# A decoder layer on one core: projection matmuls of the next unit queued on TensorE behind attention's matmuls of two steps before

## The chip, the core and the metric

The kernel runs on one core of a Trainium2 chip. Its time is the device time of one execution in microseconds (us), the median over the runs of a measurement. The engines are named as in the profile: PE (TensorE's matmuls) and PEld (its weight loads, which overlap with the matmuls), DVE (VectorE), ACT (ScalarE), POOL (GpSimd) and SP (SyncE, which issues nearly all DMAs). The order of the instructions on each engine is fixed when the program is built; an instruction that waits holds up all that stand behind it on that engine.

## What is computed

One decoder layer with 2048 tokens and a width of 1024, in float32. Of the reference this matters here:

```
proj = h @ w_in            # q,k,v of 8 forgetting ("fox") heads, q,k,v of 8 stick-breaking ("sb") heads, forget gates
o_fox = forgetting_attention(q_f, k_f, v_f, log_f)      # softmax(q.k/8 + F[t] - F[s]), s <= t
o_sb  = stick_breaking_attention(q_s, k_s, v_s)
    z = q.k/8;  rest = reversed exclusive cumsum of log_sigmoid(-z)
    a = exp(log_sigmoid(z) + rest), s < t;  o = a @ v
x = x + gate_a * (concat(head_rms_norm(o_fox), head_rms_norm(o_sb)) @ w_out)
x = x + gate_m * (silu(conv(h2 @ w_up)_gate) * conv(h2 @ w_up)_val) @ w_down
return rms_norm(x, g_final)
```

## The kernel before, in words

**Units.** The attention part is a list of 32 units (line 576): eight head pairs, first the four sb pairs, then the four fox pairs, and in each pair four blocks `tb` of 512 tokens. Below, "unit (1,2)" is the stick-breaking pair 1, token block 2, and "fox (0,2)" the forgetting pair 0, block 2. A unit's attention (`attend`, line 468) needs the unit's Q, K and V. They come from the unit's projection (`proj` and `finish_proj`, lines 341 and 283): 24 matmuls of 128x512 for q and 24 for k (line 281), and in even pairs 96 matmuls of 128x256 for the V of this pair and the next (line 320). Every product is made of three, since each factor is split in a high and a low part (`split`, line 43: a copy on ACT and a subtraction on DVE or POOL). When the accumulation of k is done, ACT copies its high part, DVE subtracts to get the low part (line 300), and four DMAs issued from SP put the two into the tile `K` (line 303). The V of odd pairs is loaded back from DRAM.

**Attention of an sb unit** goes by heads, and in a head by chunks of 512 keys from the diagonal to the left (`sb_head`, line 400). A chunk begins with the logits (two matmuls `ps_qk<-K,Q` for each of two query blocks, lines 378 and 379); the first chunk of a unit is the diagonal one, which needs the K that the unit's own projection has just made. Then ACT takes two sigmoids (410, 411), DVE a running product over the keys (the scans, 416 and 419), POOL or DVE a multiplication (420), PE transposes (388), ACT and DVE split the transposed weights (392, 393), and PE multiplies them with V (`ps_pv<-at,V`, line 397). So an sb unit goes around PE, ACT, DVE, POOL, PE, ACT, DVE, PE. A fox unit has no scans. A unit ends when DVE adds the last head's halves into `oT` (line 507).

**What sets the order.** The projection of the next unit runs beside the attention of this one. `interleave` (line 131) steps the generator `attend`, and after each step takes as many steps of `proj_gen(next unit)` as its share says (e[1] of n, line 136); what is left of the projection when attention has no more steps is drained at the end (line 142). That is the order in which the instructions are written. It is not yet the order on the engines: the program is built by a scheduler that goes by a model of the time, keeps the written order as a priority, and lets an instruction written later pass one that it takes to be still waiting. So where attention's next matmul is not ready in that model, PE is given projection matmuls, also those of the unit after the next and of the one after that, as far as the buffers go (10 tiles `hp` of activations, 5 tiles `K`, 6 tiles `V`, 2 banks for projections).

Of the kernel before, what the change touches and what calls it, by code (L numbers as in the profile page):

```python
# [1 line left out]

# [14 lines left out]
P = 128  # L17
# [16 lines left out]
def kernel(ctx: ExitStack, tc: tile.TileContext, x, c, w_ada, b_ada, g_attn, w_in, b_fgate,  # L34
                      g_out_fox, g_out_sb, w_out, g_mlp, w_up, conv_w, conv_b, w_down, g_final, out):
    nc = tc.nc
# [3 lines left out]
    def f(t):  # L40
        return t.bitcast(F32)
# [85 lines left out]
    def drain(g):  # L127
        for _ in g:
            pass

    def interleave(main, n, fillers):
        live = [[g, k, 0] for g, k, _ in fillers if g is not None]
        for i, _ in enumerate(main):
            tick()
            for e in live:
                while e[2] < (i + 1) * e[1] / n:
                    e[2] += 1
                    if next(e[0], StopIteration) is StopIteration:
                        e[2] = 1 << 30
        for g, _, whole in fillers:  # L140
            if g is not None and whole:
                drain(g)
# [3 lines left out]
    def open_pool(name, side=None, space=None):  # L146
        st = pools[name] = ExitStack()
        kw = dict(space=space) if space is not None else {}
        return st.enter_context(tc.tile_pool(name=name, bufs=1, side=side, reuse_waits="tile", **kw))
# [8 lines left out]
    sb = open_pool("sb", side="right")  # L158
# [25 lines left out]
    b = pv()  # L184
# [191 lines left out]
    def logits(cw, qcols, hl, Q, K):  # L376
        b = qk()
        nc.tensor.matmul(b[:, :cw], Q[:, hl, 0, qcols], K[:, hl, :cw], start=True, stop=False)  # L378
        nc.tensor.matmul(b[:, :cw], Q[:, hl, 1, qcols], K[:, hl, :cw], start=False, stop=True)  # L379
        return b  # L380

    def weighted(o, kts, blk, V, hl, first, last, diag):
        b = pt()
        at = sb.tile([P, 2, 2 * 2 * P], F32R, name="at", bufs=3)
        order = [(1, 0), (0, 0), (0, 1), (1, 1)]
        for i, (kk, qi) in enumerate(order):
            if not (diag and i == 0):
                nc.tensor.transpose(b[:, i * P:(i + 1) * P], blk(kts[kk], qi), ident)  # L388
        lo = P if diag else 0
        if diag:  # L390
            nc.scalar.activation(at[:, :, 0:P], edge[:, 0:2 * P].rearrange("p (a n) -> p a n", n=P), AF.Copy)
        nc.scalar.activation(at[:, 0, lo:], b[:, lo:], AF.Copy)  # L392
        nc.vector.tensor_sub(at[:, 1, lo:], b[:, lo:], f(at[:, 0, lo:]))  # L393
        for kk, kt in enumerate(kts):
            for w in range(2):
                rhs = at[:, w].rearrange("p (s q) -> p s q", q=P)[:, 0:4:3, :] if kk else at[:, w, P:3 * P]
                nc.tensor.matmul(o[:, 0:2 * P], V[kt // 4][:, kt % 4, hl, :], rhs,  # L397
                                 start=first and kk == 0 and w == 0, stop=last and kk == 1 and w == 1)

    def sb_head(j, qc, hl, Q, K, V, o):  # L400
# [61 lines left out]
    def tick(n=1):  # L462
        for d in deferred:
            d[1] -= n
        while deferred and deferred[0][1] <= 0:
            deferred.pop(0)[0]()
# [189 lines left out]
    lm = late_mod()  # L656
    Fbs = None
    tail = None
    for i, u in enumerate(units):
        kind, p, tb = u  # L660
        nxt = units[i + 1] if i + 1 < len(units) else None
        if u == ("sb", 1, 0):
            forget_sums()
        if u == ("fox", 0, 0):
            tick(1 << 20)
            close_pool("sx", "px")
            sx = open_pool("fx", side="right")
# [12 lines left out]
        if nxt is None:  # L680
            drain(lm)
            close_pool("sl", "psa")
            psc = open_pool("psc", side="right", space=PSUM)
            p2a = open_pool("p2a")
            loaded = [load_o(0, p) for p in range(3)]
            wo = []
            tail = first_mix(loaded)
        steps = nxt and (KT + 11 if nxt[:2] == ("sb", 0) else KT - 1 if nxt[1] % 2 else KT + 4)
        interleave(attend(kind, p, tb, results[kind, p], Fbs), n,
                   [(nxt and proj_gen(nxt), steps, True),  # L690
                    (lm if kind == "fox" and (p, tb) != (0, 0) else None, 4, False), (tail, 12, True)])
    drain(first_out())
    tick(1 << 20)
    for t in range(2, NTB):
# [188 lines left out]
    for sblk in range(2):  # L883
# [21 lines left out]
        a, b = bank_a(), bank_a()  # L905
# [44 lines left out]
    for tb in range(NTB):  # L950
# [12 lines left out]
        tail = []  # L963
# [57 lines left out]
```

## Time and profile before

| | us |
|---|---|
| median of 3 runs | 3142.17 |
| lowest and highest run | 3137.32, 3142.69 |
| the profiled execution | 3141.04 |
| its span from first to last instruction | 3139.3 |
| unit (0,3) of sb | 250.3 to 350.0 |
| units (1,0), (1,1), (1,2), (1,3) end at | 367.4, 404.1, 462.6, 533.9 |
| units (2,0), (2,1), (2,2), (2,3) end at | 553.2, 593.7, 653.3, 734.5 |
| units (3,0), (3,1), (3,2), (3,3) end at | 754.7, 796.7, 850.7, 922.0 |
| fox (0,0), (0,1), (0,2) end at | 959.7, 994.4, 1039.1 |
| the last fox unit ends at | 1602.0 |

The ends are those of the last `oT` addition of each unit (line 507). The rest of the span is the output projection and the channel mixer. A row of a view of stretches gives the stretch, its length, the busy time of each engine with its count of instructions, the granted TensorE clock as a share of full speed, and the share and rate of the DMA engines. A row of a timeline gives start, length, engine, line, operation, tiles and shapes, how many instructions are merged in it, and in brackets how long the engine stood idle before it and for whom. A row of waits gives who waited for whom, the total in us, how often, and the longest. Busy times of PE overlap in its pipeline, so a matmul's duration is longer than the distance from one start to the next.

### The profile page before, as it was taken

The page shows a single profiled execution, that of the slowest core. Times are in us where ns is not written, and L with a number is a line of the kernel's source. Part 1 is how long each engine was busy: PE and PEld are TensorE (multiplying, and loading weights), DVE is VectorE, ACT ScalarE, POOL GpSimd, SP SyncE. Part 2 cuts the span into 40 slices and gives each one's busy share as a digit, 9 for nine tenths or more (in the row PEclk, how much of TensorE's full clock was granted, in tenths as well). Part 3 has the DMA queues.
Part 4 walks back from the last instruction along what each step waited for, and adds up shares of the span by engine and source line. Part 5 has one row for each costly group of instructions (what it writes and reads, how often), then busy time and mean ns, then how long its engine had stood idle before and what let it go on. Part 6 is the DMA issues. An engine that isn't in the chain of part 4 may idle for free. (4 is left out here: it accounts for less than half of the span.)

```text
span 3139.3 us, 46425 instructions
## 1 busy us (share of the span) xinstructions
PE 2967.0 (95%) x15934; PEld 2511.6 (80%) x15934; DVE 2145.5 (68%) x3342; ACT 1691.0 (54%) x3161; POOL 1227.1 (39%) x1387
## 2 busy tenths in 40 slices
PE   6889998989989999999999999999899998999998
PEld 5778787877878889888877678888678887888887
DVE  6787888878875876556843587778987776354253
ACT  5666776666756676567744444444444444343332
POOL 1554455456553242242212344344444442322321
PEclk8999999999999999999999999999999999999999
DMA  9547542555336696585446632222222223554552
GB/s 267 177 140 255 168 136 69 182 185 155 123 108 221 214 314 211 158 313 162 164 158 222 212 97 86 86 83 83 82 82 89 85 81 130 190 199 161 189 199 90
DMA packets 292940, 496.51 MB, mean 158 GB/s; under 512 B 29448, under 2 KB 177664, under 8 KB 291680
## 3 DMA queue, kind: packets, MB, share of 16 engines
q1 hardware_dynamic: 281072, 480.92, 47.9%
q10 hardware_dynamic: 11632, 12.63, 1.1%
q8 instruction: 126, 2.06, 0.3%
q14 instruction: 110, 0.90, 0.1%
HBM read 352.61 MB, written 90.51 MB: 141 GB/s over the span
## 5 line engine op out<-in xcount | busy, mean ns | idle before, releaser
L810 PE MATMUL ps_o<-oa,wu 128*128 128x512 f32 x2088 | 503.5, 392 | 14.4 <-DVE oa L45 6.9
L810 PEld LDWEIGHTS ps_o<-oa,wu 128*128 128x128 f32 x2088 | 390.5, 188 | 105.5 <-DVE oa L45 10.7
L397 PE MATMUL ps_pv<-at,V 128*128 128x256 f32 x2304 | 410.9, 296 | 41.6 <-DVE at L393 24.8
L393 DVE TENSOR_TENSOR at<-ps_pt,at 128x512 fp32r<-128x512 f32 (+1 forms) x576 | 366.0, 653 | 102.8 <-ACT at L392 99.8
L281 PE MATMUL ps_pj<-hp,w_qk 128*128 128x512 f32 x1512 | 418.4, 406 | 11.1 <-ACT hp L44 3.1
L420 POOL TENSOR_TENSOR a<-a,r 128x512 f32<-128x512 f32 (+3 forms) x240 | 283.4, 1182 | 368.8 <-DVE r L416 112.3
L392 ACT ACTIVATE at<-ps_pt 128x512 fp32r<-128x512 f32 (+1 forms) x576 | 319.4, 577 | 179.8 <-PE ps_pt L388 147.3
L397 PEld LDWEIGHTS ps_pv<-at,V 128*128 128x128 f32 x2304 | 337.0, 192 | 84.6 <-DVE at L393 42.8
L281 PEld LDWEIGHTS ps_pj<-hp,w_qk 128*128 128x128 f32 x1512 | 275.7, 191 | 65.4 <-POOL hp L45 4.0
L45 DVE TENSOR_TENSOR wd<-wdraw,wd 128x1024 fp32r<-128x1024 f32 x88 | 112.4, 1277 | 261.4 <-ACT wd L44 261.4
L378 PE MATMUL ps_qk<-K,Q 128*128 128x512 f32 (+2 forms) x640 | 264.1, 414 | 11.3 <-DMA K<-q 5.8
L419 DVE TENSOR_TENSOR_SCAN r<-r 128x513 f32<-128x513 f32 x192 | 258.0, 1355 | 21.7 <-ACT r L410 14.5
L45 POOL TENSOR_TENSOR g<-graw,g 128x512 fp32r<-128x512 f32 x84 | 141.3, 1684 | 326.8 <-ACT g L44 326.8
L960 PE MATMUL ps_o<-wd,g 128*128 128x512 f32 x1040 | 250.8, 391 | 8.8 <-ACT g L44 8.8
L810 PE MATMUL ps_t<-ob,wu 128*128 128x512 f32 x984 | 243.2, 392 | 0.0
L320 PE MATMUL ps_pj<-w_v,hp 128*128 128x256 f32 (+1 forms) x1536 | 234.1, 291 | 4.8 <-DVE q L45 2.2
L379 PE MATMUL ps_qk<-K,Q 128*128 128x512 f32 (+2 forms) x640 | 238.1, 373 | 0.0
L960 PEld LDWEIGHTS ps_o<-wd,g 128*128 128x128 f32 x1040 | 196.2, 189 | 50.0 <-ACT g L44 9.2
L44 ACT ACTIVATE wu<-wuraw 128x512 fp32r<-128x512 f32 x214 | 133.2, 626 | 185.5 <-PE ps_o L810 111.5
L320 PEld LDWEIGHTS ps_pj<-w_v,hp 128*128 128x128 f32 x1536 | 211.8, 193 | 15.5 <-DVE q L45 3.1
L810 PEld LDWEIGHTS ps_t<-ob,wu 128*128 128x128 f32 x984 | 186.2, 189 | 39.4 <-DVE wu L45 0.3
L388 PE MATMUL ps_pt<-edge,a 128*128 128x128 f32 x1088 | 187.3, 281 | 27.6 <-POOL a L420 14.7
(217 smaller groups left out, 5743.3 us busy)
## 6 DMA issues: line engine op xcount, KB each, us to landing
hp<-hs SPq DMA_DIRECT2D x224, 512.0 KB
wuraw<-in_w_up_dram SPq DMA_DIRECT2D x84, 512.0 KB
wdraw<-in_w_down_dram SPq DMA_DIRECT2D x84, 512.0 KB
Q<-q SPq DMA_DIRECT2D x128, 256.0 KB
g<-u SPq DMA_DIRECT2D x42, 512.0 KB
graw<-g SPq DMA_DIRECT2D x84, 256.0 KB
hs<-hp SPq DMA_DIRECT2D x32, 512.0 KB
K<-q SPq DMA_DIRECT2D x128, 128.0 KB
```

The source lines that it names most:

```text
L45: (lo_engine or nc.gpsimd).tensor_sub(lo, src, f(hi))
L281: nc.tensor.matmul(acc, w[kt][:, a, n], h[:, bb], start=kt == 0 and i == 0, stop=kt == KT - 1 and i == 2)
L320: nc.tensor.matmul(av[:, t * width:(t + 1) * width], hts[kt][:, a, tok], w[1][kt][:, bb, 0:width], start=kt == 0 and m == 0, stop=kt == KT ...
L378: nc.tensor.matmul(b[:, :cw], Q[:, hl, 0, qcols], K[:, hl, :cw], start=True, stop=False)
L379: nc.tensor.matmul(b[:, :cw], Q[:, hl, 1, qcols], K[:, hl, :cw], start=False, stop=True)
L392: nc.scalar.activation(at[:, 0, lo:], b[:, lo:], AF.Copy)
L393: nc.vector.tensor_sub(at[:, 1, lo:], b[:, lo:], f(at[:, 0, lo:]))
L397: nc.tensor.matmul(o[:, 0:2 * P], V[kt // 4][:, kt % 4, hl, :], rhs, start=first and kk == 0 and w == 0, stop=last and kk == 1 and w == 1)
L419: nc.vector.tensor_tensor_scan(rev, rev, rev, 1.0, ALU.mult, ALU.bypass)
L420: (nc.vector if (ch + qi) % 4 == 0 else nc.gpsimd).tensor_mul(a[:, :need], a[:, :need], r[:, 1:need + 1])
L810: nc.tensor.matmul(b, w[:, p, j], o[:, q], start=first and i == 0, stop=last and i == 2, skip_group_check=True)
L960: nc.tensor.matmul(banks[t][n], g[:, a, t * P:(t + 1) * P], w[:, b, n * TB:(n + 1) * TB], start=k == 0 and i == 0, stop=k == NKD - 1 and i ...
```

## The change

While `interleave` takes steps of the fillers in a unit of the sb pairs 1, 2 and 3, each instruction that a filler puts on PE gets an edge to one matmul of attention, and so stands behind it in PE's order. That matmul is the last one that attention had issued two steps before (`marks[max(0, i - 2)]`; lines 378 to 379 and 397 note it in `latest`). The edge makes no instruction wait at run time; it binds only the order on PE. What is drained after the last step of attention gets no edge. Units of sb pair 0 and of fox stay as they were, and no instruction is added, removed or resized. Lines of the changed file from 143 on stand 5 to 8 lines further down: 281 is 288, 320 is 327, 378 and 379 are 385 and 386, 388 is 395, 397 is 404, 303 is 310.

```diff
+    latest = [None]
+
+    def interleave(main, n, fillers, paced=False):
         live = [[g, k, 0] for g, k, _ in fillers if g is not None]
+        marks = []
         for i, _ in enumerate(main):
             tick()
+            marks.append(latest[0])
             for e in live:
                 while e[2] < (i + 1) * e[1] / n:
                     e[2] += 1
-                    if next(e[0], StopIteration) is StopIteration:
+                    with tc.issue_after(marks[max(0, i - 2)].ins) if paced else nullcontext():
+                        done = next(e[0], StopIteration) is StopIteration
+                    if done:
                         e[2] = 1 << 30
...
-        nc.tensor.matmul(b[:, :cw], Q[:, hl, 1, qcols], K[:, hl, :cw], start=False, stop=True)
+        latest[0] = nc.tensor.matmul(b[:, :cw], Q[:, hl, 1, qcols], K[:, hl, :cw], start=False, stop=True)
...
-                nc.tensor.matmul(o[:, 0:2 * P], V[kt // 4][:, kt % 4, hl, :], rhs,
+                latest[0] = nc.tensor.matmul(o[:, 0:2 * P], V[kt // 4][:, kt % 4, hl, :], rhs,
...
-                    (lm if kind == "fox" and (p, tb) != (0, 0) else None, 4, False), (tail, 12, True)])
+                    (lm if kind == "fox" and (p, tb) != (0, 0) else None, 4, False), (tail, 12, True)],
+                   kind == "sb" and p > 0)
```

The built order of PE moves in the stretch from unit (0,3) to fox (0,3) and is the same, instruction for instruction, before and behind it. Three places follow, before and changed.

On PE, where unit (1,0) ends and (1,1) begins (`ps_qk<-K,Q` are logits, `ps_pj<-hp,w_qk` projections of q and k, `ps_pv<-at,V` the product with V); before:

```order
L379 MATMUL ps_qk<-K,Q 128x512
L485 MATMUL ps_pt<-headsel,sq 128x2 x2
L378 MATMUL ps_qk<-K,Q 128x512
L379 MATMUL ps_qk<-K,Q 128x512
L397 MATMUL ps_pv<-at,V 128x256 x8
L388 MATMUL ps_pt<-edge,a 128x128 x3
L378 MATMUL ps_qk<-K,Q 128x256
L379 MATMUL ps_qk<-K,Q 128x256
L378 MATMUL ps_qk<-K,Q 128x256
L379 MATMUL ps_qk<-K,Q 128x256
L388 MATMUL ps_pt<-edge,a 128x128 x4
L397 MATMUL ps_pv<-at,V 128x256 x8
```

The last row is the last product with V of unit (1,0); the logits above it are those of (1,1), three chunks of which have been begun by then. At the same place in the changed kernel:

```order
L492 MATMUL ps_pt<-headsel,sq 128x2 x2
L404 MATMUL ps_pv<-at,V 128x256 x8
L288 MATMUL ps_pj<-hp,w_qk 128x512 x18
L404 MATMUL ps_pv<-at,V 128x256 x8
L385 MATMUL ps_qk<-K,Q 128x256
L386 MATMUL ps_qk<-K,Q 128x256
L385 MATMUL ps_qk<-K,Q 128x256
L386 MATMUL ps_qk<-K,Q 128x256
L288 MATMUL ps_pj<-hp,w_qk 128x512 x6
```

Here the second `x8` is the end of unit (1,0). The 18 matmuls above it end the projection of k for unit (1,1), and the first logits of (1,1), which read that K, stand behind the end of (1,0). No logits of (1,1) stand ahead of it.

On PE, where unit (2,0) ends and (2,1) begins (`ps_pj<-w_v,hp` are projections of V); before:

```order
L397 MATMUL ps_pv<-at,V 128x256 x8
L388 MATMUL ps_pt<-edge,a 128x128 x3
L378 MATMUL ps_qk<-K,Q 128x256
L379 MATMUL ps_qk<-K,Q 128x256
L320 MATMUL ps_pj<-w_v,hp 128x256 x4
L378 MATMUL ps_qk<-K,Q 128x256
L388 MATMUL ps_pt<-edge,a 128x128 x2
L379 MATMUL ps_qk<-K,Q 128x256
L320 MATMUL ps_pj<-w_v,hp 128x256 x15
L388 MATMUL ps_pt<-edge,a 128x128 x5
L397 MATMUL ps_pv<-at,V 128x256 x8
```

Logits of (2,1), V matmuls and the last work of (2,0) stand in turn. In the changed kernel:

```order
L395 MATMUL ps_pt<-edge,a 128x128 x4
L404 MATMUL ps_pv<-at,V 128x256 x3
L327 MATMUL ps_pj<-w_v,hp 128x256 x36
L404 MATMUL ps_pv<-at,V 128x256 x8
L327 MATMUL ps_pj<-w_v,hp 128x256 x60
L385 MATMUL ps_qk<-K,Q 128x256
L386 MATMUL ps_qk<-K,Q 128x256
L385 MATMUL ps_qk<-K,Q 128x256
L386 MATMUL ps_qk<-K,Q 128x256
```

Now 96 V matmuls of unit (2,1), the whole V projection, stand between the last transposes of (2,0) and the first logits of (2,1), with only the end of (2,0) among them.

On SP, around the DMAs that fill K for unit (1,1) (`os` is the output of a finished unit, here (1,0), `hp` the next activations); before:

```order
L346 DMA hp<-hs_1_61 128x1024
L303 DMA K<-q_3908 64x512 x4
L307 DMA V<-vs_sb_2_210 128x1024
L293 DMA Q<-q_3907 64x1024 x4
L307 DMA V<-vs_sb_3_211 128x1024
```

and in the changed kernel:

```order
L353 DMA hp<-hs_1_85 128x1024
L310 DMA K<-q_3908 64x512 x2
L516 DMA os_0_112<-oT 128x512
L310 DMA K<-q_3908 64x512 x2
L300 DMA Q<-q_4285 64x1024 x4
```

The second half of K for (1,1) now stands behind the store of the output of (1,0), and the Q that follows is that of unit (1,2).

More of the change, by code (lines that the diff above doesn't have):

```diff
@@ L1 @@
-from contextlib import ExitStack
+from contextlib import ExitStack, nullcontext
 import concourse.bass as bass
@@ L129, in drain @@
             pass
-    def interleave(main, n, fillers):
+    latest = [None]
+    def interleave(main, n, fillers, paced=False):
         live = [[g, k, 0] for g, k, _ in fillers if g is not None]
+        marks = []
         for i, _ in enumerate(main):
             tick()
+            marks.append(latest[0])
             for e in live:
```

## The prediction

> **What bounds the kernel now.** I read the page first, then the stretches by unit, then the waits in the sb units.
>
> ```profile
> span 3139.3 us, 46425 instructions
> PE 2967.0 (95%) x15934; PEld 2511.6 (80%) x15934; DVE 2145.5 (68%) x3342; ACT 1691.0 (54%) x3161; POOL 1227.1 (39%) x1387
> ```
>
> Over the span PE is the busy engine. But the share is an average, and the built order of PE moves only from unit (0,3) to the start of fox (0,3). These are the sb units from (0,3) on, the three with tb = 3 in them, and fox (0,0) to (0,2):
>
> ```profile
> 250.30:922.00 671.70, 613.48 (x3867) 532.95 (x3866) 561.29 (x753) 456.00 (x997) 348.99 (x517) 0.98 0.48 150
> ...
> 462.60:533.90 71.30, 58.63 (x363) 49.20 (x362) 66.02 (x84) 49.93 (x110) 42.43 (x59) 0.95 0.28 90
> 653.30:734.50 81.20, 70.27 (x415) 58.79 (x414) 67.90 (x84) 52.77 (x114) 43.62 (x62) 0.98 0.45 146
> 850.70:922.00 71.30, 58.36 (x354) 49.23 (x353) 59.60 (x72) 45.30 (x94) 40.31 (x49) 0.95 0.28 86
> 922.00:1039.10 117.10, 113.80 (x774) 103.18 (x773) 72.39 (x198) 75.91 (x154) 41.86 (x58) 0.99 0.66 205
> ```
>
> Busy times stand in the order PE, PEld, DVE, ACT, POOL. In the fox stretch PE has 113.8 of 117.1 us and DVE 72.4: PE alone sets the time. In the sb stretch PE has 613 of 672 and DVE 561, and in the three tb = 3 units PE stands idle for 12.7, 10.9 and 12.9 us while DVE has .926, .836 and .836 of the time (66.02/71.30 and so on). That idle 36.5 us is what there is to fill. Who waits for whom in the sb stretch:
>
> ```profile
> ACT at L392 <- PE ps_pt L388: 91.3, 80, 5.3
> ...
> DVE at L393 <- ACT at L392: 33.8, 44, 4.1
> DVE oT L507 <- ACT o L506: 15.1, 11, 3.7
> ...
> PE ps_pv L397 <- DVE at L393: 21.3, 29, 1.3
> PE ps_pt L388 <- POOL a L420: 14.7, 20, 1.9
> ```
>
> It is a ring. PE waits for DVE and POOL, DVE for ACT, and ACT for PE. No wait is long, since the attention of a unit overlaps with that of the next: PE's order at the end of (1,0) has logits of (1,1) ahead of the last product with V.
>
> **The change part by part.** Its own run took 3141.0 us (3139.3 of span and 1.7 around it), 1.1 under the median 3142.2. I sum against 3141.0. No instruction is added; what changes is where 189 projection matmuls stand, and what stands at the units' ends.
>
> *Work that goes from sb to fox.* I counted the projection matmuls in PE's order by unit. From (0,3) to (3,3) 712 of q and k and 589 of V stand before, 624 and 488 in the changed order. So 88 and 101 go over to fox (0,0) to (0,2). Two runs and the groups of the page price them:
>
> ```profile
> 344.73 3.34 PE L281 MATMUL ps_pj<-hp,w_qk 128*128 128x512 f32 x14
> ...
> 544.15 1.82 PE L320 MATMUL ps_pj<-w_v,hp 128*128 128x256 f32 x14
> ...
> L281 PE MATMUL ps_pj<-hp,w_qk 128*128 128x512 f32 x1512 | 418.4, 406 | 11.1 <-ACT hp L44 3.1
> ...
> L320 PE MATMUL ps_pj<-w_v,hp 128*128 128x256 f32 (+1 forms) x1536 | 234.1, 291 | 4.8 <-DVE q L45 2.2
> ```
>
> A run of 14 lasts 13 distances and one duration: (3.34 - .41)/13 = .225 us for q and k, (1.82 - .29)/13 = .118 for V. 88 x .225 + 101 x .118 = 19.8 + 11.9 = 31.7 us, and at the fox stretch's 117.1 us for 113.8 of PE, **+33 us** there. Nothing hides it; PE is full. Before, this work lay under DVE's time in sb.
>
> *What sb gives back.* PE loses 31.7 us there, but DVE keeps its 561 us; few of its instructions change sides. So the length is 561.3 over the share that DVE can have, plus the stretches in which the new order leaves it nothing. The share is bounded by the units in which PE was not full: at best .926 as in (1,3), 606 us; at worst .865, the three tb = 3 units together (193.52/223.80), 649 us. Two things pull: fewer long rows of projections ahead of attention's transposes help (ACT's 91.3 us of waiting), and the tb = 3 units, now with 139 projection matmuls in (1,3) and (3,3) in place of 50 and 60, come to look like (2,3), which had 95 and .836. I take the middle, .895, 627 us: **-45 us** against 671.7.
>
> *The new ends of units: K.* In the changed order the k projection of (1,1) ends just ahead of the last eight products with V of (1,0), and the first logits of (1,1) stand right behind those. The trace shows one such chain, at the first unit:
>
> ```profile
> 60.62 0.60 ACT L44 ACTIVATE q<-ps_qk 128x512 fp32r<-128x512 f32 x1 [0.26 <-PE ps_qk L281]
> ...
> 63.27 0.68 DVE L45 TENSOR_TENSOR q<-ps_qk,q 128x512 fp32r<-128x512 f32 x1
> ...
> 65.80 2.30 SPq L303 DMA_DIRECT2D K<-q  x2
> ...
> 70.15 0.39 PE L378 MATMUL ps_qk<-K,Q 128*128 128x256 f32 x1 [3.59 <-DMA K<-q]
> ...
> 70.69 0.28 ACT L410 ACTIVATE r<-ps_qk 128x128 f32<-128x128 f32 x1 [1.68 <-PE ps_qk L379]
> ...
> 71.07 0.43 DVE L416 TENSOR_TENSOR_SCAN r<-r,edge 128x129 f32<-128x129 f32 x1 [3.04 <-ACT r L410]
> ```
>
> The copy takes .60, the subtraction .68, two issues 2.30, and the last of them lands after 70.15 - 68.10 = 2.05 us; then .54 to the sigmoid and .38 to the first scan. That is 5.6 us from the last k matmul to the logits, 6.5 to DVE's scan. Ahead of the waiting logits on PE stand only the eight products with V (1.11 us):
>
> ```profile
> 360.20 1.11 PE L397 MATMUL ps_pv<-at,V 128*128 128x256 f32 x8
> ```
>
> Behind them six projection matmuls, held by the edge, and all of (1,1). On SP the second half of K also stands behind the store of `oT`, under 1 us more. So PE stands 4.5 us and DVE, which has the K subtraction and one `oT` in that time, about 5. The order has this at four ends, into (1,1), (1,2), (3,1) and (3,2). Into (1,3), (3,0) and (3,3) PE has 3.4 to 4.7 us of work between the last k matmul and the first logits, but no logits stand ahead of the last product with V either: 3 us each. 4 x 5 + 3 x 3 = **29 us**; at least half is sure, by the missing overlap alone.
>
> *The new ends of units: V.* In pair 2 the V projections that are left when attention has no more steps are drained together, ahead of the next unit's attention in the written order. Into (2,1) 96 of them stand between the last transposes and the first logits, 96 x .118 = 11 us in which DVE gets only the V splits; into (2,2) 68, 8 us; into (2,3) 25, 3 us. Together **22 us**. So in even pairs V is not spread at all.
>
> *The clock.* In unit (1,0) the granted clock was .93 of full, though no single wait of PE in it was longer than 1.15 us:
>
> ```profile
> 350.00:367.40 17.40, 15.05 (x84) 12.48 (x83) 14.41 (x26) 12.73 (x33) 6.52 (x17) 0.93 0.95 303
> ...
> 364.32 0.44 PE L388 MATMUL ps_pt<-edge,a 128*128 128x128 f32 x2 [1.15 <-DVE at L393]
> ```
>
> .07 of 17.4 is 1.2 us of PE's clock lost. With 1.2 at each of the ten new ends, 12 at most, and nothing where DVE sets the pace behind them, I put **+3**. The Trainium skill, "TensorE: Matmul & The Clock Gate", Part 1, says that the clock halves after an idle window of about 3.4 us; by that the four K ends alone would halve it, once each, which is an estimate of 4 x 1.7 = 7 us in place of the 3. The row here shows a loss behind a shorter wait, and the measurement decides.
>
> The sum: 33 - 45 + 29 + 22 + 3 = +42. **3141 + 42 = 3183 us.** With the best share and all else it is 3141 + 33 - 66 + 51 = 3159; with the worst share and the clock at 12, 3141 + 33 - 23 + 51 + 12 = 3214.
>
> **The rivals.**
>
> *The gaps close (faster).* PE is the engine with most to do, its idle 36.5 us in the tb = 3 units get the projections, and the next unit's logits find their K in time because the edges bind order only and the steps before were spread. For it: PE's 95%, and that (1,3) had only 50 projection matmuls. Then DVE runs at .926 with no stretches lost: 33 - 66 = -33, 3108 us. Against it: DVE has .926 in (1,3) already, so a filled PE there gains little; and the order shows the ends. The Trainium skill, "Perfetto Trace Analysis", Identifying the Most-Contended Engine, says to take the engine of highest occupancy and to optimize it first; by that this rival is the likely one. It decides if DVE's idle time per unit end stays under 1 us.
>
> *The gain and the loss meet.* The share is .926 and only half of the 51 us at the ends is lost: 33 - 66 + 26 = -7, 3134 us; a little more loss, and it is no change at all.
>
> *Much slower.* The share falls to .836, that of (2,3) and (3,3), since the edges keep PE from running ahead in every unit: 561.3/.836 = 671 us, so 33 + 0 + 51 + 12 = +96, 3237 us. Against it: ACT's and DVE's waits behind long rows of projections get fewer.
>
> That the change does nothing is excluded, since the order differs over sixteen units.
>
> **How the numbers follow.** A measurement of this kernel can tell about 0.2%, 6 us, from no change. I give my forecast, 3150 to 3218, a chance of .74; the gaps closing .08; the meeting .11, of which .08 counts as within 0.2% and .03 as faster; much slower .07. So faster .11, same .08, slower .81. The range leaves out the closed gaps and the much slower case, 1.5 in 10: 3134 to 3218. The likeliest time is that of the sum, 3183.
>
> **What would show it.** In the changed profile: the stretch from the end of (3,3) to the end of fox (0,2) some 33 us longer, PE full in it; a wait of PE for `DMA K<-q` of 3 to 5 us at four ends of units, 12 to 20 us together, where the sb stretch now has none so long; DVE idle for about 10 us across the end of (2,0), with PE in a row of V matmuls; and sb from 250 us on between 660 and 700 us long. I am wrong if the sb stretch is under 640 us: then DVE had the projections to thank for its waits, and the ends cost little. I am wrong in the first term if the fox stretch grows by less than 25 us.

## The result and the profile after

| | before | changed |
|---|---|---|
| median, us | 3139.74 | 3273.99 |
| lowest and highest, us | 3136.12, 3142.69 | 3270.84, 3277.67 |
| ratio, with its 95% interval | | 1.0422 (1.0408 to 1.0435) |

The change makes the kernel slower by 134 us, 4.2%. The sign was forecast; the size was not: 3183 was given, with 3134 to 3218 as the range. The busy times are the same work in a longer span, from the page of the changed kernel:

```profile
span 3275.9 us, 46402 instructions
...
PE 3019.5 (92%) x15934; PEld 2543.3 (78%) x15934; DVE 2158.4 (66%) x3342; ACT 1689.5 (52%) x3162; POOL 1239.2 (38%) x1387
```

The span grew by 136.6 us. Two stretches hold nearly all of it: sb from the end of (0,2) to the end of (3,3), and fox (0,0) to (0,2). The changed kernel's view of stretches (length, then PE, PEld, DVE, ACT, POOL, clock, DMA share and rate):

```profile
250.70:1022.70 772.00, 629.80 (x3680) 535.48 (x3679) 564.43 (x745) 450.25 (x990) 361.38 (x517) 0.91 0.39 119
1022.70:1169.20 146.50, 143.63 (x952) 129.62 (x950) 77.15 (x201) 77.95 (x160) 42.17 (x58) 1.00 0.72 229
```

sb is 100.3 us longer with the same 561 to 564 us of DVE work. Fox is 29.4 longer, with PE full and 178 more matmul records. The rest of attention adds 3 us, and what follows it 3.5.

Where in sb is it? I cut a stretch of 20 us, from 8 before to 12 behind the end of each unit from (1,0) to (3,2), eleven stretches, and asked for the busy times in them. In the changed kernel, the end of (3,0) and the sum of the eleven:

```profile
809.40:829.40 20.00, 9.90 (x40) 8.31 (x40) 3.32 (x7) 3.49 (x10) 1.11 (x5) 0.67 0.64 206
...
sum 220.00, PE 154.74 PEld 132.96 DVE 81.58 ACT 78.28 POOL 42.67; mean PE 14.07 PEld 12.09 DVE 7.42 ACT 7.12 POOL 3.88
```

The same sum in the kernel before:

```profile
sum 220.00, PE 210.15 PEld 187.07 DVE 186.09 ACT 159.55 POOL 112.66; mean PE 19.10 PEld 17.01 DVE 16.92 ACT 14.50 POOL 10.24
```

DVE stands idle for 138.4 of the 220 us, before for 33.9: **104.5 us more, which is all that sb lost**. Outside of these stretches DVE's idle time fell from 76.5 to 69.2 us, and its own work grew by 3.1 (104.5 - 7.3 + 3.1 = 100.3). No engine of the ring got more to do; they stand and wait. In the end of (3,0) all four engines of the ring are idle for half of the time and more; before, the same end reads:

```profile
746.70:766.70 20.00, 18.43 (x112) 15.43 (x111) 14.49 (x23) 15.01 (x38) 15.01 (x24) 1.00 0.57 138
```

What they wait for there, by the waits of the changed kernel in sb:

```profile
ACT r L417 <- PE ps_qk L386: 110.5, 61, 12.7
...
DVE r L423 <- ACT r L417: 61.0, 14, 12.7
PE ps_qk L385 <- DMA K<-q: 54.4, 7, 12.3
...
DVE r L426 <- ACT r L417: 34.1, 22, 4.1
...
DVE V L45 <- ACT V L44: 16.7, 13, 3.0
```

Before, DVE's first scan waited 6.4 us for ACT in all of sb, and no row there has PE waiting for K:

```profile
DVE r L416 <- ACT r L410: 6.4, 10, 2.1
```

Now PE waits for K seven times, up to 12.3 us, and ACT's sigmoid and DVE's scan wait behind it. One of the seven, the end of (1,1), in the changed kernel's timeline:

```profile
395.86 12.04 SPq L353 DMA_DIRECT2D hp<-hs  x8
...
404.64 2.91 PE L288 MATMUL ps_pj<-hp,w_qk 128*128 128x512 f32 x12
...
407.39 1.11 PE L404 MATMUL ps_pv<-at,V 128*128 128x256 f32 x8
407.58 0.60 ACT L44 ACTIVATE q<-ps_pj 128x512 fp32r<-128x512 f32 x1 [2.32 <-PE ps_pj L288]
408.21 1.46 SPq L310 DMA_DIRECT2D K<-q  x2
408.22 0.69 DVE L45 TENSOR_TENSOR q<-ps_pj,q 128x512 fp32r<-128x512 f32 x1 [2.54 <-ACT q L44]
...
410.49 1.29 SPq L310 DMA_DIRECT2D K<-q  x2
417.85 0.58 PE L385 MATMUL ps_qk<-K,Q 128*128 128x256 f32 x1 [9.36 <-DMA K<-q]
...
419.13 1.17 DVE L423 TENSOR_TENSOR_SCAN r<-r,edge 128x129 f32<-128x129 f32 x2 [9.76 <-ACT r L417]
```

The last k matmuls of the projection stand just ahead of the last product with V, as the forecast had it. But eight loads of `hp` are issued ahead of K, and the last DMA of K, issued by 411.78, is not there before 417.85: 6.1 us. The forecast had taken 2.05 from the first unit. There only four DMAs of Q, 256 KB each, stood between the halves of K and two loads of weights, 128 KB each, just ahead of it; a load of `hp` has 512 KB. The loads of weights in the kernel before:

```profile
59.43 0.84 SPq L256 DMA_DIRECT2D raw_v<-in_w_in_dram  x2
```

At the end of (1,1) DVE is idle for 9.8 us.

### The profile page after: what moved, and what is told of

Same layout as the page of the kernel before. It is cut to its first block, busy times and chain, and to the rows that moved or that the text cites. A ratio compares the mean times of both kernels' runs of the same rounds, so it can differ in the third digit from the quotient of the medians.

```text
span 3275.9 us, 46402 instructions
## 1 busy us (share of the span) xinstructions
PE 3019.5 (92%) x15934; PEld 2543.3 (78%) x15934; DVE 2158.4 (66%) x3342; ACT 1689.5 (52%) x3162; POOL 1239.2 (38%) x1387
## 5 line engine op out<-in xcount | busy, mean ns | idle before, releaser
L404 PE MATMUL ps_pv<-at,V 128*128 128x256 f32 x2304 | 421.4, 302 | 49.7 <-DVE at L400 28.2
L288 PE MATMUL ps_pj<-hp,w_qk 128*128 128x512 f32 x1512 | 425.8, 417 | 7.6 <-ACT hp L44 3.0
L288 PEld LDWEIGHTS ps_pj<-hp,w_qk 128*128 128x128 f32 x1512 | 288.6, 200 | 65.1 <-POOL hp L45 4.0
L385 PE MATMUL ps_qk<-K,Q 128*128 128x512 f32 (+2 forms) x640 | 271.4, 425 | 72.1 <-DMA K<-q 60.1
L426 DVE TENSOR_TENSOR_SCAN r<-r 128x513 f32<-128x513 f32 x192 | 265.0, 1388 | 49.7 <-ACT r L417 34.8
L417 ACT ACTIVATE r<-ps_qk 128x512 f32<-128x512 f32 (+2 forms) x320 | 174.4, 545 | 148.7 <-PE ps_qk L386 119.4
L386 PE MATMUL ps_qk<-K,Q 128*128 128x512 f32 (+2 forms) x640 | 242.4, 380 | 0.0
L327 PE MATMUL ps_pj<-w_v,hp 128*128 128x256 f32 (+1 forms) x1536 | 225.8, 290 | 1.7 <-DVE q L297 1.7
```

Of the source, the lines that this page charges most:

```text
L288: nc.tensor.matmul(acc, w[kt][:, a, n], h[:, bb], start=kt == 0 and i == 0, stop=kt == KT - 1 and i == 2)
L327: nc.tensor.matmul(av[:, t * width:(t + 1) * width], hts[kt][:, a, tok], w[1][kt][:, bb, 0:width], start=kt == 0 and m == 0, stop=kt == KT ...
L386: latest[0] = nc.tensor.matmul(b[:, :cw], Q[:, hl, 1, qcols], K[:, hl, :cw], start=False, stop=True)
L404: latest[0] = nc.tensor.matmul(o[:, 0:2 * P], V[kt // 4][:, kt % 4, hl, :], rhs, start=first and kk == 0 and w == 0, stop=last and kk == 1 ...
L426: nc.vector.tensor_tensor_scan(rev, rev, rev, 1.0, ALU.mult, ALU.bypass)
```

## The experiments

Three explanations were put against each other, and the expectations call them by letters. A: the loss is made at the ends of units, above all by K that comes late behind the loads on SP. B: those loads matter little. C: the edges slow attention inside the units. Later two more came: E, that the lower clock behind the long waits costs time, against F, that it costs none; and G, that the missing overlap of two units is enough by itself. All diffs are against the changed kernel. A time is compared with the kernel before on the same chip, whose median was 3144 to 3147 us there (3140 on the chip of the result above), so ratios are safer to compare between runs than times. All kernels compute the whole layer.

**The loads behind K, in all units.**

```diff
...
-                nc.sync.dma_start(f(K[r * HD:(r + 1) * HD, h]), f(k2[h * HD:(h + 1) * HD, r]))
+                last_k[0] = nc.sync.dma_start(f(K[r * HD:(r + 1) * HD, h]), f(k2[h * HD:(h + 1) * HD, r]))
...
-            nc.sync.dma_start(f(h), hs[tb][kt])
+            with tc.issue_after(last_k[0].ins):
+                nc.sync.dma_start(f(h), hs[tb][kt])
```

> Edit: in the changed kernel, the loads of the activations hp for a projection stand on SP behind the DMAs that fill K of the projection before. The result after the change is 3274.0 us; in its trace PE waits 54.4 us for K at seven unit ends, 4 to 12 us each, where 3 to 5 us were forecast, and up to eight hp loads of 512 KB are issued on SP in the 12 us ahead of K. Theory A (queue): K's packets stand behind those of the hp loads in the same queue, so a landing takes 6 us and not 2. Then the waits for K fall to about 3 to 4 us each, 20 to 28 us together, and the time to 3230 to 3248. Rival B (the missing overlap alone): the ends cost what they cost because no logits stand ahead of them, and K lands late whatever stands in the queue. Then the waits stay over 45 us and the time is within 3262 to 3282.

3273.29 us, ratio 1.041 (1.039 to 1.0431): no gain in all. But sb fell by 31 us to 741.1, and PE's waits for K in it from 54.4 to 24.6 us; the edge also held the loads in fox, where the three units and those behind them grew by 24 us together. The run had mixed two things and decided nothing, so it was repeated with the edge in sb alone.

**The loads behind K, in sb alone.**

```diff
...
-            nc.sync.dma_start(f(h), hs[tb][kt])
+            with tc.issue_after(last_k[0].ins) if kind == "sb" and (p, tb) > (1, 0) else nullcontext():
+                nc.sync.dma_start(f(h), hs[tb][kt])
```

> Edit: as the run in which the hp loads stand behind K on SP, but only for the sb projections from (1,1) on; the fox projections load as in the changed kernel. In that run the waits for K fell from 57.8 to 27.9 us and the sb stretch from 771.9 to 741.1 us, as the queue theory had it, while fox, where the loads were held too, grew by 24 us and hid it. Theory A (queue): the sb gain stays and fox is as in the changed kernel, so 3274 - 31 = 3238 to 3250. Rival: the later hp loads of sb cost elsewhere what K gains, 3265 to 3276.

3250.86 us, ratio 1.0337 (1.0321 to 1.0354). Its stretch of sb, its wait for K, and the end of (1,1) in its timeline:

```profile
251.70:999.20 747.50, 627.57 (x3678) 532.75 (x3677) 574.59 (x744) 452.48 (x990) 369.76 (x517) 0.92 0.40 122
```

```profile
PE ps_qk L387 <- DMA K<-q: 30.6, 6, 9.4
```

```profile
406.24 1.10 SPq L311 DMA_DIRECT2D K<-q  x2
...
408.01 1.11 SPq L311 DMA_DIRECT2D K<-q  x2
409.22 4.09 SPq L355 DMA_DIRECT2D hp<-hs  x8
...
410.96 0.55 PE L387 MATMUL ps_qk<-K,Q 128*128 128x256 f32 x1 [4.56 <-DMA K<-q]
```

With the loads behind it, K is there 410.96 - 409.12 = 1.84 us after its last issue, in place of 6.1. sb is shorter by 24.5 us. A had 31 in mind, and the time is 0.9 us above its range, but far from that of its rival; B falls. So the loads ahead of K on SP cost some 24 us of the 134. Whether K waits there for its turn in the queue or for bytes that the same DMA engines move, this run does not tell apart. Four fifths of the loss are still there.

**Projections at twice the pace.** The filler takes its steps in the first half of the unit, so that K is made long before the end.

```diff
-                while e[2] < (i + 1) * e[1] / n:
+                while e[2] < (i + 1) * e[1] * (2 if paced else 1) / n:
```

> Edit: in the changed kernel the paced projections are stepped twice as fast, so that k ends near the middle of the unit, V at three quarters, and nothing is left to be drained at the unit's end. In the order the first logits of most units again stand ahead of the last product with V of the unit before, except into (1,1) and (3,1), and 40 matmuls of q and k and 64 of V go from sb to fox in place of 88 and 101, which is 16.6 us and not 31.7. Theory (ends): what the change lost it lost at the ends of units, 88 us of DVE's idle time around K and 24 us around V. Then the waits for K fall to under 20 us and the time to 3165 to 3195. Rival C (edges): the edges slow attention inside the units, since PE may not run ahead; then only the fox share and V come back, and the time is 3225 to 3250.

3220.88 us, ratio 1.0246 (1.0221 to 1.0271), between what the two had given. PE stands waiting for DMAs for long only at the two ends into (1,1) and (3,1), 6.95 and 6.79 us (the first is put down to the store of `oT`, which is issued right behind K's DMAs). sb is still 48 us longer than before (719.8 us), so a loss of another kind is there, without a late K.

**Pair 2 alone, and pairs 1 and 3 alone.** In pair 2 the ends get rows of V matmuls, in pairs 1 and 3 the late K.

```diff
-                   kind == "sb" and p > 0)
+                   kind == "sb" and p == 2)
```

> Edit: only the units of pair 2 are paced. In the order the k of (2,1) to (3,0) ends 14 us of PE work or more ahead of its logits, so no wait for K is expected, and sb and fox keep their projection matmuls (712 and 589 in sb, as before the change). What is left is the rows of V matmuls at the ends of (2,0), (2,1) and (2,2). Theory (ends): DVE stands about 8 us at each, so 24 us over the kernel before, 3155 to 3170. Rival D: PE works in that time and is the engine with most to do, so the rows cost nothing and the spread in (2,3) gains; 3125 to 3143.

```diff
-                   kind == "sb" and p > 0)
+                   kind == "sb" and p in (1, 3))
```

> Edit: the units of pairs 1 and 3 are paced, not those of pair 2. The order has the late k into (1,1), (1,2), (1,3), (3,1), (3,2) and (3,3), and 88 and 101 matmuls go from sb to fox as with the whole change, but no row of V at unit ends but short ones, and the k of (3,0) ends 37 us ahead. Theory (ends): the loss is that of the whole change less the V rows (24 us) and the end into (3,0) (10 us): 3233 to 3248. Rival C (edges): the loss goes with the number of paced units, 8 of 12: 30 us for fox and two thirds of 104, 3230 at the most and rather 3220.

Pair 2 alone: 3174.32 us, 1.0103 (1.0085 to 1.0121). Pairs 1 and 3 alone: 3259.52, 1.0371 (1.0352 to 1.039). Both came out above what I had given, and pair 2 has no late K at all. Fox tells them apart: 115.3 us with pair 2 alone, as before, and 146.4 with pairs 1 and 3. So the 29 us in fox come from pairs 1 and 3. The run with the tb = 3 units alone, below, has them too, which leaves (1,3) and (3,3); only (3,3) lies next to fox.

**Only the tb = 3 units.** They are the ones in which PE had idle time to fill.

```diff
-                   kind == "sb" and p > 0)
+                   kind == "sb" and p > 0 and tb == 3)
```

> Edit: only the units with tb = 3 of pairs 1, 2 and 3 are paced, those in which PE stood idle for 36.5 us before the change. In the order no k ends late (17 us of PE work or more ahead of its logits), 88 matmuls of q and k and 101 of V go from sb to fox as with the whole change, and (1,3) and (3,3) have 133 projection matmuls in place of 50 and 60. Theory: fox costs 30, the ends nothing, the tb = 3 units grow by 5 to 8 us each as their projections do not fit beside a busy DVE, and the emptier units ahead of them give back about 30: 3144 plus 5 to 25. Rival: the idle time of PE is really filled, and the time falls below 3138.

3191.72 us, ratio 1.0145 (1.013 to 1.016), above both expectations. sb and fox in its view of stretches:

```profile
251.70:933.80 682.10, 598.05 (x3678) 512.27 (x3677) 564.23 (x744) 450.57 (x989) 368.33 (x517) 0.96 0.43 134
933.80:1080.60 146.80, 144.12 (x952) 129.65 (x950) 77.14 (x201) 78.06 (x160) 42.16 (x58) 1.00 0.73 229
```

The three units did get shorter, 69.7, 75.7 and 69.6 us against 71.3, 81.2 and 71.3: 8.8 us in all. That is what filling PE's gaps there brings in this run. Against it stand fox with its whole 30 us, and (2,0), (2,1) and (3,0), longer by 8.6, 8.4 and 12.9: PE's order has no logits of theirs ahead of the end of the unit before. No wait for K is left in sb. The loss needs no late K.

**The same edges, one unit later.** Each projection matmul stands behind the matmul of the unit before at the same share of that unit, so the spreading stays, but next unit's projection may run a unit ahead and the overlap at the ends comes back.

```diff
...
-                    with tc.issue_after(marks[max(0, i - 2)].ins) if paced else nullcontext():
+                    with tc.issue_after(earlier[0][i * len(earlier[0]) // n].ins) if paced else nullcontext():
...
+        earlier[0] = marks
```

> Edit: in place of the matmul of two steps before, the edge goes to the matmul at the same share of the unit before. So the projections may run one whole unit ahead and no further. In the order the logits of each unit again stand 7 to 16 us of PE work ahead of the end of the unit before, the last k matmul stands 13 us or more ahead of its logits, the tb = 3 units have 49 to 210 projection matmuls, and only 34 of q and k go from sb to fox (7.7 us). Theory (ends): without late K and rows of V nothing is lost but the 8 us in fox; 3144 to 3160. Rival C (edges): spreading itself slows attention in the units, as the 139 and more projection matmuls in (1,3) and (3,3) do; 3165 to 3190. If spreading fills PE's idle time in the tb = 3 units at no cost, the time is under 3138.

3146.59 us, ratio 1.0003 (0.9994 to 1.0012). Its sb and fox:

```profile
251.00:902.70 651.70, 604.59 (x3831) 528.86 (x3830) 570.67 (x752) 454.80 (x997) 366.26 (x517) 0.97 0.49 149
902.70:1036.10 133.40, 125.08 (x811) 112.38 (x809) 73.78 (x200) 77.01 (x155) 42.25 (x58) 0.96 0.67 211
```

sb is 20 us shorter than before, not longer. So spreading by edges does no harm inside the units. The edges of the changed kernel bind closer, but there DVE's idle time outside of the ends fell as well, from 76.5 to 69.2 us: C falls. DVE has .876 of the stretch (570.67/651.70), the most of all twelve runs. What is won is given back in fox, 16 us.

**The missing overlap alone.** The projections get no edges, as before. Instead the first step of attention of each unit from (1,1) on gets an edge to the last product with V of the unit before, so its logits can't stand ahead of that.

```diff
+    def behind(main, held):
+        with tc.issue_after(latest[0].ins) if held else nullcontext():
+            first = next(main)
+        yield first
+        yield from main
+
...
-        for i, _ in enumerate(main):
+        for i, _ in enumerate(behind(main, paced)):
...
-                    with tc.issue_after(marks[max(0, i - 2)].ins) if paced else nullcontext():
-                        done = next(e[0], StopIteration) is StopIteration
+                    done = next(e[0], StopIteration) is StopIteration
...
-                   kind == "sb" and p > 0)
+                   kind == "sb" and (p, tb) > (1, 0))
```

> Edit: the projections run ahead freely, as before the change; instead, the first logits of each unit from (1,1) to (3,3) get the edge, to the last product with V of the unit before. In the order no logits stand ahead of a unit's end at these eleven ends, as in the changed kernel, while the last k matmul stands 60 us of PE work or more ahead of its logits and sb keeps its 712 and 589 projection matmuls. So K is never late, no row of V must be drained, nothing goes to fox: what is left is the missing overlap alone. Theory G (the emptied ring): each end costs about 5 us or more, since the ring of PE, ACT, DVE and POOL runs empty and fills again; eleven ends, 55 to 80 us, 3200 to 3226. Rival A (only late K and the rows of V cost): within 15 us of the kernel before, 3146 to 3161.

3229.28 us, ratio 1.0263 (1.0237 to 1.0288), 3 us above what G had given: **84.5 us for eleven ends, 7.7 us each**. Its sb and fox, and the sum of its eleven stretches:

```profile
250.70:1005.10 754.40, 649.62 (x3868) 556.07 (x3867) 576.17 (x754) 456.12 (x997) 370.55 (x517) 0.94 0.43 134
1005.10:1123.20 118.10, 114.12 (x774) 103.36 (x773) 72.44 (x199) 76.06 (x154) 41.75 (x58) 0.99 0.65 203
```

```profile
sum 220.00, PE 197.10 PEld 167.29 DVE 115.97 ACT 110.15 POOL 79.54; mean PE 17.92 PEld 15.21 DVE 10.54 ACT 10.01 POOL 7.23
```

Fox is as before, and no row of its waits has PE waiting for K. DVE is idle for 104.0 us at the eleven ends, 70.1 more than before, 6.4 for each. Another 15 us of the longer sb are DVE's own busy time, for the same work. Two thirds of them lie in the long scans, before and in this run:

```profile
L419 DVE TENSOR_TENSOR_SCAN r<-r 128x513 f32<-128x513 f32 x168 | 222.9, 1338 | 20.3 <-ACT r L410 13.8 <-POOL r L418 3.5 <-POOL r L415 1.2
L429 DVE TENSOR_TENSOR_SCAN r<-r 128x513 f32<-128x513 f32 x168 | 233.5, 1400 | 30.7 <-ACT r L420 21.6 <-POOL r L428 8.3
```

By the starts and ends in the traces, such a scan takes 1.22 us in both runs where POOL is busy for less than 0.1 us of it, and 1.57 and 1.60 where POOL is busy for over 1 us of it; before there are 57 of the second kind, here 80. So these scans are longer because more of them run beside POOL's work, as far as records that go together can show it. The end of (1,1) in its timeline shows how the ring runs empty:

```profile
412.01 2.34 PE L291 MATMUL ps_pj<-hp,w_qk 128*128 128x512 f32 x9 [1.03 <-DVE q L45]
...
414.19 0.76 PE L407 MATMUL ps_pv<-at,V 128*128 128x256 f32 x5
...
414.78 2.23 PE L291 MATMUL ps_pj<-hp,w_qk 128*128 128x512 f32 x9
...
416.85 0.52 PE L407 MATMUL ps_pv<-at,V 128*128 128x256 f32 x3
...
417.20 0.28 PE L388 MATMUL ps_qk<-K,Q 128*128 128x256 f32 x1
...
417.68 4.95 PE L291 MATMUL ps_pj<-hp,w_qk 128*128 128x512 f32 x21
...
417.81 0.42 DVE L517 TENSOR_TENSOR oT<-ps_pv,o 64x256 f32<-64x256 f32 x1 [3.90 <-ACT o L516]
...
418.26 1.38 DVE L426 TENSOR_TENSOR_SCAN r<-r,edge 128x129 f32<-128x129 f32 x2
...
422.47 0.39 PE L388 MATMUL ps_qk<-K,Q 128*128 128x512 f32 x1
...
423.88 2.35 DVE L429 TENSOR_TENSOR_SCAN r<-r 128x513 f32<-128x513 f32 x2 [4.24 <-ACT r L420]
```

PE is never idle for long here. The scheduler gave it projections where attention had nothing ready: 18 among the last products with V, 21 behind the first logits. DVE has nothing to scan ahead of the end (3.90 us), only two rows of 129 after it, and the next chunk's logits come 5 us later (4.24 us). So the 84.5 us are the price of ends without overlap together with the order that the scheduler then finds, the longer scans and a clock of .94 in place of .98; drain and refill were not taken apart.

**Pair 2 without the drained V.** Pair 2 alone, with more steps of the filler, so that V is not left for the end.

```diff
-        steps = nxt and (KT + 11 if nxt[:2] == ("sb", 0) else KT - 1 if nxt[1] % 2 else KT + 4)
+        steps = nxt and (KT + 11 if nxt[:2] == ("sb", 0) else KT - 1 if nxt[1] % 2 else KT + 10 if p == 2 and kind == "sb" else KT + 4)
...
-                   kind == "sb" and p > 0)
+                   kind == "sb" and p == 2)
```

> Edit: as the run with pair 2 alone paced, which was 30 us over the kernel before, but with all the steps of the V projections taken inside the unit, so that no row of V matmuls is left to be drained at its end; logits of (2,2) and (2,3) again stand 10 us of PE work ahead of the end of the unit before. Theory (ends): the rows of V cost the 22 to 30 us; 3144 to 3156. Rival C (edges): the edges slow the attention in pair 2; 3165 to 3176 again.

3165.19 us, ratio 1.0063 (1.005 to 1.0076), 9 us less than pair 2 alone. The theory had given 3144 to 3156; the time lies at the lower bound of its rival, by which the edges slow the attention in pair 2. The lengths of the units do not bear that rival out. (2,2) and (2,3) came back to 60.9 and 77.2 us, but (2,1) and (3,0) still take 50.5 and 30.0 against 40.5 and 20.2 before. By the trace their first logits are issued on PE only 0.6 us or less ahead of the last products with V of the unit before, so there is next to no overlap at these two ends. About 10 us for each of them remain, with no wait of PE for K over 2.0 us and no drained row; at the end of (2,0), though, some 80 V matmuls now stand inside the last 14 us of the unit.

**Warm matmuls.** Six more matmuls of constants, which nothing reads, stand on PE between the last product with V and the first logits at the seven ends with a late K, so that its clock does not fall while it waits.

```diff
...
+        if warm:
+            b = pj()
+            with tc.issue_after(latest[0].ins):
+                for _ in range(warm):
+                    nc.tensor.matmul(b, edge[:, 0:P], edge[:, 0:TB], start=True, stop=True)
...
-                   kind == "sb" and p > 0)
+                   kind == "sb" and p > 0,
+                   6 if kind == "sb" and p > 0 and nxt[1] % 2 else 0)
```

> Edit: in the changed kernel six added 128x512 float32 matmuls of constants, whose result nothing reads, stand on PE at the seven late-K ends between the last product with V and the first logits, where PE waits 4 to 12 us for K. In the changed kernel the clock was at half for 143 us of the sb stretch, before the change for 24. Theory E (clock): PE's half clock after the waits slows the refilling of the ring of PE, ACT, DVE and POOL; with PE kept busy the half-clock time in sb falls under 115 us and the time by 10 to 25 us, to 3249 to 3264. Rival F: the ring waits for DVE and POOL behind the waits, and the clock costs nothing; 3272 to 3282, with the added matmuls that outlast the shorter waits.

3277.64 us, ratio 1.0418 (1.04 to 1.0435), the same as the change. Its sb and its group of warm matmuls (each counts twice there):

```profile
249.20:1015.50 766.30, 657.68 (x3763) 542.00 (x3763) 565.91 (x745) 450.17 (x990) 364.04 (x517) 0.93 0.39 119
```

```profile
L154 PE MATMUL ps_pj<-edge 128*128 128x512 f32 x84 | 38.7, 611 | 0.0
```

The clock rose from .91 to .93 in sb: by the trace it was at half for 102 us in place of 143, so the clock lost 51 us in place of 72. These 20 us of clock bought no time. F holds as far as the run goes. It goes less far than it seems: a part of the regained clock fell to the added matmuls themselves, and at three of the seven ends PE no longer waits for K at all, so that the added matmuls may hold the logits back a little there.

**Two versions that might win.** The edges one unit later, only where they do not push work into fox: pairs 1 and 2 in the one, all but unit (3,3) in the other.

```diff
...
-                   kind == "sb" and p > 0)
+                   kind == "sb" and p in (1, 2))
```

> Edit: as the run in which the edge goes to the same share of the unit before, but only in the units of pairs 1 and 2. There sb was 19.9 us shorter than before the change and the three fox units 16.3 us longer, with no difference in all. With pair 3 free to run ahead the order again has 712 and 589 projection matmuls in sb, as before the change. Theory: the loss in fox is the work moved there, so fox is back at 117 us and two thirds of the gain in sb stay: 13 us under the kernel before, a ratio of 0.994 to 0.998. Rival: gain and loss are one thing, PE work pushed to later units; then the ratio is 0.999 to 1.002 again.

```diff
...
-                   kind == "sb" and p > 0)
+                   kind == "sb" and p > 0 and (p, tb) != (3, 3))
```

> Edit: as the run in which the edge goes to the same share of the unit before, but without unit (3,3), in which the projection of fox (0,0) is written. The order again has 712 and 589 projection matmuls in sb. Theory: fox is back at 117 us and nearly all of the 20 us in sb stays, 0.992 to 0.997 of the kernel before. Rival: the gain in sb came from the work that went to fox; 0.999 to 1.002.

3136.21 us, ratio 0.9972 (0.9963 to 0.9982), and 3136.49, 0.997 (0.996 to 0.998). Both beat the kernel before by some 10 us, 0.3%, and the changed one by some 140, going by the ratios. The second one's sb and fox, and the sum of its eleven stretches:

```profile
250.30:912.10 661.80, 608.02 (x3867) 530.24 (x3867) 569.78 (x754) 455.84 (x997) 364.21 (x517) 0.98 0.50 153
912.10:1028.50 116.40, 112.44 (x774) 101.98 (x773) 72.63 (x199) 75.54 (x154) 41.73 (x58) 1.00 0.67 206
```

```profile
sum 220.00, PE 208.14 PEld 182.57 DVE 186.96 ACT 155.47 POOL 109.17; mean PE 18.92 PEld 16.60 DVE 17.00 ACT 14.13 POOL 9.92
```

sb keeps its 3867 matmuls, fox its 774, DVE is idle for 33 us at the ends as before, and 10 us are won.

## Why the prediction was wrong in its size

The forecast's terms, and what the trace of the changed kernel has for each. For the ends it is DVE's idle time in the 20 us around each, less that of before; the missing overlap's column is the same difference in the run with the missing overlap alone:

| term | forecast, us | changed kernel | missing overlap alone |
|---|---|---|---|
| work from sb to fox | +33 | +29.4 | +1.0 |
| K: ends into (1,1), (1,2), (3,1), (3,2) | +20 | +50.6 | +26.4 |
| K: ends into (1,3), (3,0), (3,3) | +9 | +26.3 | +21.5 |
| V: ends into (2,1), (2,2), (2,3) | +22 | +22.2 | +17.9 |
| the end into (2,0) | 0 | +5.4 | +4.3 |
| the rest of sb (the DVE share) | -45 | -4.2 | +12.6 |
| clock | +3 | in the rows above | in the rows above |
| rest of attention, and behind it | 0 | +6.6 | not split |
| sum | +42 | +136.3 | |

*Work from sb to fox: right.* PE was full there, nothing hid it, and each run that left the 774 matmuls in fox had it back at 115 to 118 us. The Trainium skill, "Perfetto Trace Analysis", Optimization Strategy, says that a kernel whose most contended engine changes with time may gain when the stretches of different kind are interleaved. The trace agrees, the other way round: PE has 113.8 of 117.1 us in fox and 613 of 672 in sb, and the 31.7 us of work moved across that border the wrong way cost 29.4.

*The step that failed first: the price of an end, "3 us each" and "4 x 5".* The mechanism was named, and the seven ends with a late K are the ones that the order showed. But they cost 76.9 us in place of 29, for two reasons. The forecast took the overlap of two units for a small part of an end, "at least half is sure, by the missing overlap alone", that is 15 us. That overlap alone, with K in time, costs 47.9 at these seven ends and 84.5 us of the kernel's time at all eleven: no row of before had priced it, since there every end had its overlap, and DVE idles 3 us there. I had counted the chain from the last k matmul to the scan (6.5 us) as if the ring then went on at full pace; it first has to fill again, with two short rows to scan before the next chunk's logits. The second reason is K's landing. The 2.05 us came from a place with no load of `hp` ahead of K on SP; with eight ahead it is 6.1, and they are worth 24 us in the run that moved them. The Trainium skill, "DMA: Bandwidth & Descriptors", Queues, rings and completion order, says that DMAs issued from one engine share its rings, that descriptors are taken in ring order, and that a DMA's completion lands only after the earlier writes of the same DMA engine; the two landings here, 6.1 and 1.84 us, agree. The prediction named SP among the queues, but counted only the store of `oT` ahead of K and not the loads.

*The step that failed next: "-45".* It let DVE's share rise from .836 to .895 by filling PE's idle time and by shorter rows. In the changed kernel the time outside of the ends gave back 4. Three runs say how much there was to have: filling the three tb = 3 units gives 8.8 us there, the edges one unit later 20 in all of sb, at a share of .876, and the winning version 10. With 4 us given back the share, in the sense of the forecast, is 561.3/667.5 = .841, under the worst bound in the text, .865. As I read it, PE's idle time in the tb = 3 units was mostly that of a ring whose other engines had not got there yet, and not a place where DVE lacked matmuls; no run shows that apart.

*V: right in its number, in part by luck.* It is 22.2 for 22, but the forecast took it from the length of the V rows on PE. The missing overlap alone gives 17.9 at the same three ends, with no row to be drained, and with no drained row pair 2 alone loses only 9 us less.

*The clock: a small term that came out large in the rows and nil in time.* It fell to .91 in sb, 72 us of clock against 12 before, but the run with warm matmuls shows no gain from raising it.

*The rivals.* "The gaps close" and "the gain and the loss meet" fell. "Much slower", 3237, was the nearest in size, and its share of .836 was close to the .841; but it had the edges slow attention in every unit. DVE's idle time outside of the ends fell, and the edges one unit later made sb shorter: that mechanism is refuted. "What would show it" gave sb 660 to 700 us and 12 to 20 us of waiting for K; 772 and 54 were the first sign in the trace that the ends were mis-sized.

*The three parts together.* Measured one by one, the missing overlap (84.5 us), the loads ahead of K (24) and the work in fox (29) make 138 of the 134 us. That the sum fits so well is partly chance: some 15 of the 84.5 are DVE's longer busy time, of which the changed kernel has 3, and no run has all three parts in and out in turn.

*Still open:* how the 7.7 us of an end without overlap divide between drain, refill and the longer scans; and why fox grew by 16 us with the edges one unit later, though only some 35 more q and k matmuls, 8 us, are in it.

## What to carry to other kernels

Where a unit's work goes around a ring of engines, price an order by what stands across the unit's end: if the next unit's first instruction can't stand ahead of the last one of this unit, the ring empties and fills again, here 7.7 us each time with all that follows from it, and no wait or busy share of the kernel before shows that price. Before binding filler to a place in the stream, ask of it what the scheduler was doing with the freedom: here it ran a unit ahead, and the same spreading bound to the unit before kept that and won 10 us, where it moved no work into fox. For a small transfer on which the critical engine waits, read what is issued ahead of it on its queue, at the place where it will stand.

## What the runs showed of the hardware

The four small DMAs of K landed 6.1 us after their last issue with eight loads of `hp` ahead of them, and 1.84 us with the loads behind. The granted clock was .67 in the 20 us around the end of (3,0) and .79 and .78 at the ends of (1,1) and (1,0), where PE waited for K, and .91 over sb against .98 before. The Trainium skill, "TensorE: Matmul & The Clock Gate", Part 1, has the clock halve after an idle window of some 3.4 us; the trace agrees that it falls there. What I had not expected is that 20 us of it, given back by warm matmuls, changed the time by nothing that shows. That fits a ring that waits for other engines than PE there; the runs do not show it apart.

A 128x513 scan on DVE took 1.22 us with POOL idle beside it and 1.57 with POOL busy for over 1 us of it, in the kernel before; the run with the missing overlap alone has 1.22 and 1.60.
